# The 16 by 16 substitution of a chunked RWKV-7 kernel, on GpSimd instead of VectorE

## The chip, the cores and the metric

The kernel runs on one core of a Trainium2 chip. The metric is the device time of one execution in microseconds (us), the median over several runs. A core has five engines that run side by side, each taking its own instructions in order: TensorE (PE in the profile; PEld is its loading of weights), VectorE (DVE), ScalarE (ACT), GpSimd (POOL) and SyncE (SP), which here only issues DMAs. The order within each engine's queue is settled when the program is built; between engines semaphores keep the data right.

## The reference

One layer of a hybrid diffusion backbone over 256 latent and 256 context tokens of width 2048, all in float32. A modulated RMS norm is followed by one input projection, whose columns go to an RWKV-7 branch that runs over the tokens in both directions, to a latent attention branch, and to gates. Both branches are projected back, merged by sigmoid gates, projected once more and added to the input. The change lies in the RWKV-7 branch, which per head and direction runs this recurrence over tokens:

```
def rwkv7_step(S, xs):
    r, w, k, v, kk, akk = xs
    sa = einsum("dbhij,dbhj->dbhi", S, -kk)
    S = S * w[..., None, :] + sa[..., :, None] * akk[..., None, :] + v[..., :, None] * k[..., None, :]
    return S, einsum("dbhij,dbhj->dbhi", S, r)
```

There are 16 heads of 64 channels. The recurrence starts at zero, runs through the context, and then from the state reached through the latent tokens.

## The kernel before, in words

The input projections are matrix products in float32 split into a high and a low part (three products for one): ScalarE casts the high part `wh` of a loaded weight tile `w`, VectorE subtracts to get `wl`, and the products go to PSUM as `acc`. The weights come in 512 KB loads on SP's queue into three buffers, and the split halves into three buffers each (`weights`, lines 210 to 219).

The recurrence is done in chunks of 64 tokens. Within a chunk it needs the inverse of a triangular 64 by 64 matrix for each head and direction. The heads go in eight pairs, and each pair in two halves, first the 256 context tokens and then the 256 latent ones, so there are 16 halves. One half has eight chunks counting both directions, two heads, and four diagonal blocks of 16 by 16 in each matrix: 64 blocks. Four generators work on the halves:

- `front(h)` (lines 646 to 813) prepares decays and keys and the triangular products `AQ`, mostly on VectorE and ScalarE (tiles `En`, `Ep`, `th`, `km`, `BK`, `QR` or `Qbd`).
- `diagonal(h, AQ, WT)` (lines 815 to 852) inverts the diagonal blocks. Eight DMAs bring the blocks of `AQ` to DRAM (`dl`, line 821), another brings them back as `ln` with one block to a partition: 64 partitions of 256 elements. Two copies put them into the first half of the tile `wt`, called `X`, those of the backward direction transposed. Then come 14 steps, each with one multiplication into `pr` and one addition into `X`, on 64 partitions and k times (15 - k) elements (14 to 56), and a memset writes the unit diagonal. ScalarE writes the transposed blocks into the other half of `wt` (line 839). One DMA takes both to DRAM (`dw`, line 842), and eight bring them to their places in `WT` (line 848). There is one buffer for `wt`, and `pr` uses the buffer of `ln`.
- `back(h)` (lines 858 to 977) forms the whole inverse from the diagonal blocks with four rounds of products in PSUM tile `lv`, the first two of which read `WT`, and then goes through the chunks with small products (`chp`) and copies (`xs`, `UV`, `Mn`) on ScalarE and VectorE.
- `final(p, Y)` normalizes the result.

In between, a background of input projections (`bg_k`, `bg_r`, `bg_z`, `merge_gate_g` and others) fills TensorE. The order in which all this is written into the program comes from `drive` (lines 505 to 538), a planner with a clock: `Elementwise` objects (lines 110 to 123) stand for VectorE (`V`) and ScalarE (`S`); a call advances the engine's time by elements per partition/rate plus a fixed part (line 121) and sets when a chain's next step may be placed. `diagonal` also gives fixed waits for its DMAs (`LT`, line 60), and `back(h)` is not begun before `diagonal(h)` is through. The instructions of the substitution are written under `tc.high_priority(HS)`, by which the tile framework puts them ahead of others in their engine's queue as soon as they can run.

After the RWKV-7 stage come latent attention, the branch projections and the output projection; they do not use the substitution.

Of the kernel before, what the change touches and what calls it, by code (L numbers as in the profile page):

```python
# [13 lines left out]
ALU = mybir.AluOpType  # L14
# [112 lines left out]
def hybrid_block(  # L127
# [20 lines left out]
    nc = tc.nc  # L148
    clock = Clock()
    V, S = Elementwise(nc.vector, clock, 960, 0.066), Elementwise(nc.scalar, clock, 1200, 0.08)  # L150
    E = Tensor(nc.tensor, clock)
    PSUM = bass.MemoryType.PSUM

# [10 lines left out]
    def con(name):  # L164
        o, w = CO[name]
        return cc[:, o:o + w]
# [54 lines left out]
    def mm3(ps, ah, al, bh, bl, start, stop):  # L221

        E.matmul(ps, lhsT=ah, rhs=bh, start=start, stop=False)
        E.matmul(ps, lhsT=ah, rhs=bl, start=False, stop=False)
        E.matmul(ps, lhsT=al, rhs=bh, start=False, stop=stop)

# [16 lines left out]
    with tc.tile_pool(name="p1", bufs=2) as p1:  # L243
# [20 lines left out]
        def mod_a(k):  # L264

            pm = pp.tile([P, 512], F32, name="pm", tag="ch")
            for r, wm in enumerate(load_mod(k)):
                for g in range(4):
                    E.matmul(pm[32 * g:32 * g + 32, 0:256], lhsT=ssil[:, 4 * r + g], rhs=wm[:, g],
                             start=r == 0, stop=r == 3, tile_position=(0, 32 * g))  # L270
# [4 lines left out]
        def mod_b(k):  # L275

            pm, part = parts.pop(k)
            for i in range(2):
                E.transpose(pm[:, 256 + 128 * i:384 + 128 * i], part[:, 128 * i:128 * i + 128], ident)
            mod = p1.tile([P, 4], F32, name="mod", tag="mod", bufs=4)  # L280
# [10 lines left out]
        for k in range(KT):  # L291
# [3 lines left out]
            else:  # L295
                V.tensor_tensor(sq, xT[:, k], xT[:, k], ALU.mult)
            g = k % 4
            E.matmul(pst[32 * g:32 * g + 32], lhsT=con("ones")[:, 0:32], rhs=sq, start=k < 4, stop=k >= KT - 4,
                     tile_position=(0, 32 * g))
# [205 lines left out]
    def drive(chains, *queues, dens=0.0, lf=1.0, lat=0.0):  # L505

        clock.t = clock.ready = V.t = S.t = 0.0
        chains = [[g, 0.0, None] for g in chains]  # L510
        while chains or any(queues):
            for q in queues:
                if q and not any(c[0] is q[0] for c in chains):
                    chains.append([q[0], clock.t, None])
            for c in chains:
                if c[2] is not None and c[2]():
                    c[2] = None
                    c[1] = max(c[1], clock.t)
                if c[2] is None and clock.t >= c[1] and (clock.density(WIN) >= dens or not (main or extra)):
                    clock.ready = clock.t  # L520
                    r = next(c[0], "end")
                    if r == "end":
                        chains.remove(c)
                        for q in queues:
                            if q and c[0] is q[0]:
                                q.pop(0)
                    else:
                        c[1] = clock.t + lf * (clock.ready - clock.t) + lat
                        if callable(r):
                            c[2] = r  # L530
                        else:
                            c[1] += r or 0.0
                    break
            else:
                t = clock.ready = clock.t
                next(bg, None)
                if clock.t == t:
                    clock.t += 0.2
# [11 lines left out]
    with tc.tile_pool(name="rw", bufs=1) as rw:  # L550
# [95 lines left out]
        def front(h):  # L646
# [104 lines left out]
            else:  # L751
                for d in range(2):
# [6 lines left out]
                    yield  # L759

            lanes.append(diagonal(h, AQ, WT))


# [51 lines left out]
        def diagonal(h, AQ, WT):  # L815

            dl = dram.tile([8, 8, 16, 16], F32, name="dl", tag="dl")
            for g in range(2):
                for b in range(4):
                    r0 = 64 * g + 16 * b  # L820
                    nc.sync.dma_start(dl[:, 4 * g + b].rearrange("u r c -> r u c"), AQ[r0:r0 + 16, g, :, 16 * b:16 * b + 16])
            yield LT[0]
            ln = rw.tile([64, 16, 16], F32, name="ln", tag="ln")
            nc.sync.dma_start(ln.rearrange("p r c -> p (r c)"), dl.rearrange("u h r c -> (u h) (r c)"))
            yield LT[1]
            with tc.high_priority(HS):
                wt = rw.tile([64, 2, 16, 16], F32, name="wt")
                X = wt[:, 0]
                V.tensor_copy(X[0:32], ln[0:32])
                V.tensor_copy(X[32:64], ln[32:64].rearrange("p r c -> p c r"))  # L830
                pr = rw.tile([64, 16, 16], F32, name="pr", tag="ln")
                for k in range(14, 0, -1):

                    m = 15 - k
                    V.tensor_tensor(pr[:, 0:k, 0:m], X[:, 0:k, k:k + 1].to_broadcast([64, k, m]),
                                    X[:, k, k + 1:16].unsqueeze(1).to_broadcast([64, k, m]), ALU.mult)
                    V.tensor_tensor(X[:, 0:k, k + 1:16], X[:, 0:k, k + 1:16], pr[:, 0:k, 0:m], ALU.add)
                V.memset(X.rearrange("p r c -> p (r c)")[:, 0:256:17], 1.0)
                S.copy(wt[:, 1], X.rearrange("p r c -> p c r"))
            dw = dram.tile([2, 8, 8, 16, 16], F32, name="dw", tag="dw")  # L840
            yield LT[2]
            nc.sync.dma_start(dw.rearrange("w u h r c -> (u h) w (r c)"), wt.rearrange("p w r c -> p w (r c)"))
            yield LT[3]
            WTu = WT.rearrange("p w u t -> p (w u) t")
            for g in range(2):
                for b in range(4):
                    r0 = 64 * g + 16 * b
                    nc.sync.dma_start(WTu[r0:r0 + 16, :, 16 * b:16 * b + 16],
                                      dw[:, :, 4 * g + b].rearrange("w u r c -> r (w u) c"))
            yield LT[4]  # L850
            nonlocal inverted
            inverted += 1
# [205 lines left out]
        def back_chain():  # L1058
            nonlocal backs
            for h in range(2 * NPAIR):  # L1060
                yield (lambda: fronts > h and inverted > h)
                yield from back(h)
                backs += 1

        drive([back_chain(), front_chain()], finals, lanes, dens=DENS, lf=LF, lat=LATX)
        while ("q", 3) not in done:
            next(bg)
# [447 lines left out]
```

## Time and profile before

| What | Value |
|---|---|
| Median of 3 runs | 1336.67 us (1335.77 to 1337.12) |
| The profiled execution, its own time | 1337.52 us |
| Its span in the profile | 1335.6 us |
| ScalarE busy | 618.8 us, 46% |
| GpSimd busy | 3.3 us, 9 instructions |
| Mean granted TensorE clock | 0.981 |
| First and last substitution instruction | 172.4 us and 904.0 us |

The page of a profile gives the busy time of each engine in one execution, a timeline in 40 slices, the chain of work that ended last, and the costliest groups of instructions: line, engine, operation, out<-in by the names of the tiles, shapes, count, busy time, mean duration in ns, idle time of the engine just before them and what ended it. Most rows have L122 or L103, since all vector, scalar and matrix operations are issued through helpers there; so tiles tell them apart. Further views give the busy time in chosen windows, who waited for whom, the instructions of one tile, and the instructions in order of time. Matmuls are pipelined and their ends are modelled.

### The profile page before, as it was taken

The numbers are of one execution on the slowest core, as the hardware profiler recorded it, in microseconds if no ns is written. First come the engines' busy times: TensorE is split into PE (matmuls) and PEld (weight loads), VectorE is DVE, ScalarE is ACT, GpSimd is POOL, SyncE is SP. The second block draws the span as 40 slices with busy tenths as digits, with TensorE's granted clock in tenths as the row PEclk, the third lists the DMA queues.
The fourth block names the chain that finished last, engine by engine and source line by source line (L and its number), as shares of the span: only waits on it lengthen the run. The fifth ranks groups of instructions, "written<-read, shape, count | busy, mean of one in ns | idle before, by whom it ended". The sixth has DMA issues, their size and how long they took to land.

```text
span 1335.6 us, 29638 instructions
## 1 busy us (share of the span) xinstructions
PE 1273.5 (95%) x11484; PEld 1057.0 (79%) x11484; DVE 958.0 (72%) x2704; ACT 618.8 (46%) x1370; POOL 3.3 (0%) x9
## 2 busy tenths in 40 slices
PE   5999989999999998999999999999989999799998
PEld 2667877788787787788787777788878888799887
DVE  4445878878777868677876887776548877677655
ACT  3445544444443544344444444544436665444443
POOL 0000000000000000000000000000000000000000
PEclk9999999999999999999999999999979999899999
DMA  9995554354352454254254232353344332577685
GB/s 380 417 418 206 181 164 130 89 171 142 78 173 64 123 163 127 56 166 132 57 110 125 72 99 80 93 151 100 107 150 123 103 103 95 189 227 234 188 270 174
DMA packets 127740, 208.12 MB, mean 156 GB/s; under 512 B 63600, under 2 KB 80752, under 8 KB 127088
## 3 DMA queue, kind: packets, MB, share of 16 engines
q1 hardware_dynamic: 127600, 206.23, 49.0%
q8 instruction: 90, 1.47, 0.5%
q14 instruction: 50, 0.41, 0.1%
HBM read 193.33 MB, written 12.85 MB: 154 GB/s over the span
## 4 chain that ended last, share of the span: by engine, by line
PE 79%; DVE 11%; DMA 6%; issue 2%; ACT 2%; SPq 0%; DVEq 0%; ACTq 0%
PE acc L103 33%; PE chp L103 17%; PE lv L103 10%; PE wk L103 6%; PE a L103 5%; PE ch L103 3%; DMA w<-in_w_proj 3%; DVE wl L122 3%; PE wk L107 2%; PE pm L103 2%; DMA wm<-in_w_mod_ss 2%; DVE BK L122 1%; ACT wh L122 1%; DVE wt L122 1%; DMA xT<-in_xcT 1%
## 5 line engine op out<-in xcount | busy, mean ns | idle before, releaser
L122 ACT CAST wh<-w 128x512 fp32r<-128x512 f32 (+1 forms) x484 | 289.1, 607 | 336.3 <-PE acc L103 182.5
L122 DVE TENSOR_TENSOR wl<-w,wh 128x512 fp32r<-128x512 f32 (+1 forms) x480 | 319.7, 674 | 134.1 <-ACT wh L122 123.8
L103 PE MATMUL acc<-hmh,wh 128*128 128x256 f32 (+1 forms) x1200 | 390.6, 325 | 0.0
L103 PE MATMUL acc<-hml,wh 128*128 128x256 f32 (+2 forms) x1200 | 370.3, 309 | 0.8 <-issue 0.8
L103 PE MATMUL acc<-hmh,wl 128*128 128x256 f32 (+1 forms) x1184 | 364.6, 308 | 0.6 <-DVE wl L122 0.5
L103 PEld LDWEIGHTS acc<-hmh,wh 128*128 128x128 f32 x1200 | 228.0, 190 | 28.7 <-issue 6.8
L103 PEld LDWEIGHTS acc<-hmh,wl 128*128 128x128 f32 x1184 | 225.3, 190 | 14.9 <-DVE wl L122 1.1
L103 PEld LDWEIGHTS acc<-hml,wh 128*128 128x128 f32 (+1 forms) x1200 | 228.0, 190 | 11.0 <-issue 0.8
L122 DVE TENSOR_TENSOR pr<-wt 64x14 f32<-64x14 f32 (+6 forms) x224 | 42.5, 190 | 4.7
L122 DVE TENSOR_TENSOR wt<-wt,pr 64x14 f32<-64x14 f32 (+6 forms) x224 | 42.3, 189 | 4.3
L122 ACT COPY UV<-Mn 64x128 f32<-64x128 f32 x112 | 33.1, 295 | 22.1 <-DVE Mn L122 18.4
L103 PE MATMUL chp<-ob0h,wh 128*128 128x256 f32 x128 | 37.4, 293 | 5.7 <-ACT ob0h L122 5.7
L103 PEld LDWEIGHTS chp<-UV,AQ 128*64 128x64 f32 (+1 forms) x512 | 24.5, 138 | 21.3 <-ACT UV L122 10.9
L103 PE MATMUL a<-hmh,wh 128*128 128x512 f32 x96 | 40.7, 424 | 0.0
L122 ACT COPY UV<-chp 64x128 f32<-64x128 f32 x64 | 16.5, 257 | 50.8 <-PE chp L103 50.6
L103 PE MATMUL chp<-UV,AQ 128*64 128x64 f32 (+1 forms) x512 | 35.9, 238 | 4.2 <-ACT UV L122 4.1
L103 PE MATMUL a<-hmh,wl 128*128 128x512 f32 x96 | 38.1, 397 | 0.4 <-DVE wl L122 0.4
L103 PE MATMUL a<-hml,wh 128*128 128x512 f32 x96 | 37.9, 395 | 0.0
L103 PE MATMUL chp<-ob0l,wh 128*128 128x256 f32 x128 | 37.4, 292 | 0.0
L122 DVE SCALAR_TENSOR_TENSOR Mn<-chp,rho,Mr 128x64 f32<-128x64 f32 x96 | 24.1, 278 | 18.2 <-PE chp L103 17.7
L103 PE MATMUL chp<-ob0h,wl 128*128 128x256 f32 x128 | 37.1, 290 | 0.0
L103 PE MATMUL chp<-ob1h,wh 128*128 128x256 f32 x128 | 36.5, 285 | 0.0
(324 smaller groups left out, 2388.1 us busy)
## 6 DMA issues: line engine op xcount, KB each, us to landing
w<-in_w_proj SPq DMA_DIRECT2D x148, 512.0 KB, 3.8
wm<-in_w_mod_ss SPq DMA_DIRECT2D x64, 512.0 KB, 9.4
w<-in_w_mod_g SPq DMA_DIRECT2D x32, 512.0 KB, 3.6
w<-in_w_br SPq DMA_DIRECT2D x32, 512.0 KB, 3.6
w<-in_w_out SPq DMA_DIRECT2D x32, 512.0 KB, 3.7
w<-in_w_first SPq DMA_DIRECT2D x16, 384.0 KB, 8.5
xT<-in_xcT SPq DMA_DIRECT2D x4, 1024.0 KB, 8.6
thd<-th SPq DMA_DIRECT2D x32, 128.0 KB, 1.8
```

Source lines behind the costliest of these rows:

```text
L103: return self.engine.matmul(out, lhsT=lhsT, rhs=rhs, **kw)
L107: return self.engine.transpose(*a)
L122: return fn(out, *a, **kw)
```

## The change

The planner gets a third `Elementwise` object, `G`, for GpSimd, with VectorE's rate and fixed part. The two copies, the 28 multiplications and additions and the memset of each substitution are issued through it. ScalarE's transposing copy, the DMAs, the tiles and their buffers, the priority and the fixed waits stay.

```
+    G = Elementwise(nc.gpsimd, clock, 960, 0.066)
...
-        clock.t = clock.ready = V.t = S.t = 0.0
+        clock.t = clock.ready = V.t = S.t = G.t = 0.0
...
-                V.tensor_copy(X[0:32], ln[0:32])
-                V.tensor_copy(X[32:64], ln[32:64].rearrange("p r c -> p c r"))
+                G.tensor_copy(X[0:32], ln[0:32])
+                G.tensor_copy(X[32:64], ln[32:64].rearrange("p r c -> p c r"))
                 pr = rw.tile([64, 16, 16], F32, name="pr", tag="ln")
                 for k in range(14, 0, -1):
                     m = 15 - k
-                    V.tensor_tensor(pr[:, 0:k, 0:m], X[:, 0:k, k:k + 1].to_broadcast([64, k, m]),
+                    G.tensor_tensor(pr[:, 0:k, 0:m], X[:, 0:k, k:k + 1].to_broadcast([64, k, m]),
                                     X[:, k, k + 1:16].unsqueeze(1).to_broadcast([64, k, m]), ALU.mult)
-                    V.tensor_tensor(X[:, 0:k, k + 1:16], X[:, 0:k, k + 1:16], pr[:, 0:k, 0:m], ALU.add)
-                V.memset(X.rearrange("p r c -> p (r c)")[:, 0:256:17], 1.0)
+                    G.tensor_tensor(X[:, 0:k, k + 1:16], X[:, 0:k, k + 1:16], pr[:, 0:k, 0:m], ALU.add)
+                G.memset(X.rearrange("p r c -> p (r c)")[:, 0:256:17], 1.0)
                 S.copy(wt[:, 1], X.rearrange("p r c -> p c r"))
```

## The prediction

> **What bounds the kernel now.** I began with the page: the span, busy time by engine, then the costliest groups.
>
> ```profile
> span 1335.6 us, 29638 instructions
> ...
> PE 1273.5 (95%) x11484; PEld 1057.0 (79%) x11484; DVE 958.0 (72%) x2704; ACT 618.8 (46%) x1370; POOL 3.3 (0%) x9
> ...
> L122 DVE TENSOR_TENSOR pr<-wt 64x14 f32<-64x14 f32 (+6 forms) x224 | 42.5, 190 | 4.7
> L122 DVE TENSOR_TENSOR wt<-wt,pr 64x14 f32<-64x14 f32 (+6 forms) x224 | 42.3, 189 | 4.3
> ```
>
> TensorE bounds the kernel, and GpSimd does nothing after its first memsets. The work that moves is 448 small VectorE instructions of 0.19 us. Taking it off an engine that is 72% busy gains only what TensorE now waits for because of it. So the next view was busy time by window: all of the stage from the first substitution to the last, and then the sixteen stretches in which a substitution runs, one per half (a half is one pair of heads with the context or the latent tokens).
>
> ```profile
> 172.40:904.00 731.60, 704.50 (x7293) 576.38 (x7293) 567.87 (x1742) 326.45 (x782) 0.00 (x0) 0.98 0.41 116
> ```
>
> ```profile
> 172.40:190.30 17.90, 13.79 (x119) 12.07 (x119) 15.80 (x61) 6.29 (x13) 0.00 (x0) 0.90 0.58 170
> ...
> 250.50:264.80 14.30, 14.08 (x135) 10.82 (x132) 13.27 (x47) 8.43 (x21) 0.00 (x0) 1.00 0.25 76
> ...
> 343.20:354.80 11.60, 11.26 (x161) 8.78 (x161) 10.45 (x43) 4.67 (x11) 0.00 (x0) 1.00 0.16 48
> ...
> 483.90:496.50 12.60, 12.60 (x129) 11.47 (x129) 10.89 (x44) 4.99 (x11) 0.00 (x0) 1.00 0.67 206
> ...
> 691.00:706.70 15.70, 11.94 (x109) 10.63 (x108) 9.65 (x41) 4.49 (x11) 0.00 (x0) 0.92 0.53 109
> 757.60:768.00 10.40, 10.40 (x136) 8.09 (x134) 9.51 (x40) 4.72 (x10) 0.00 (x0) 1.00 0.09 35
> ...
> sum 222.70, PE 212.43 PEld 177.25 DVE 196.70 ACT 99.67 POOL 0.00; mean PE 13.28 PEld 11.08 DVE 12.29 ACT 6.23 POOL 0.00
> ```
>
> After each window's length come the busy times of PE, PEld, DVE, ACT and POOL. VectorE is 196.70/222.70 = 88% busy in these stretches and (567.87 - 196.70)/(731.60 - 222.70) = 73% outside them, so it is crowded where the substitution runs. TensorE is idle 222.70 - 212.43 = 10.3 us in all sixteen: 4.1 in the first, 3.8 in the one from 691, where VectorE itself is idle 6 us and so isn't the cause, and 2.4 in the other fourteen. A substitution takes 222.70/16 = 13.9 us on average, though its own instructions are much shorter: it is interleaved with other VectorE work.
>
> **What it removes.** The tile that the substitution works on shows all its instructions:
>
> ```profile
> L122 DVE COPY wt<-ln x32: 271/324/381, 172.4 to 890.6; 32x256 f32<-32x256 f32 x32
> L122 DVE MEMSET wt<- x16: 72/72/72, 174.3 to 892.5; 64x16 f32 x16
> ```
>
> Per half VectorE loses 28 x 0.19 + 2 x 0.324 + 0.072 = 6.0 us, 97 us over 16 halves. What TensorE gets of that I take from the first stretch, where one wait makes up the whole loss.
>
> ```profile
> 181.91 0.70 PE L103 MATMUL wk<-QR,BK 64*128 64x128 f32 x4 [4.11 <-DVE pr L122]
> ```
>
> ```profile
> 181.09 0.67 DVE L122 TENSOR_TENSOR QR<-cr,Ep 128x512 f32<-128x512 f32 x1
> ```
>
> ```profile
> 172.40:181.09 8.69, 2.43 (x13) 0.00 (x0) 1.00 0.60 182
> ```
>
> The matmul needs the QR tile, whose last part VectorE starts at 181.09. Up to there the instructions that read or write the substitution's tile took 2.43 us of VectorE (this window counts them alone). With them gone QR is ready 2.4 us earlier, and the wait falls from 4.1 to 1.7. The next thing late there is the rest of VectorE's own queue. I take the same share, 2.43/4.11 = 0.59, of the 2.4 us idle in the fourteen other stretches: 1.4. The 3.8 of the stretch from 691 stay. Gain: 2.4 + 1.4 = 3.8 us, bounded above by 10.3 (all the idle time) and below by zero if nothing else happens.
>
> **What it adds.** GpSimd runs 31 instructions per half, most of which wait for the one before. No operation with an input runs on GpSimd in this trace; its memsets are the nearest rows.
>
> ```profile
> L554 POOL MEMSET WT<- 128x1024 f32 x2 | 1.8, 954 | 127.0 <-PE a L103 127.0
> ...
> L562 POOL MEMSET restart<- 128x260 f32 x1 | 0.3, 313 | 0.0
> L563 POOL MEMSET restart<- 128x4 f32 x1 | 0.1, 104 | 0.1
> ```
>
> A memset of 16 elements would take 0.104 + 12 x (0.313 - 0.104)/256 = 0.114 us here, against 0.072 on VectorE. Lower bound: 28 x 0.114 + 2 x 0.313 + 0.114 = 3.9 us for the substitution. Estimate: VectorE's two-input instruction takes 0.190/0.072 = 2.6 times its memset, so on GpSimd 0.30 us. For the handing over between dependent instructions I read VectorE where nothing stands between two of them:
>
> ```profile
> 694.05 0.20 DVE L122 TENSOR_TENSOR wt<-wt,pr 64x44 f32<-64x44 f32 x1
> 694.28 0.20 DVE L122 TENSOR_TENSOR pr<-wt 64x50 f32<-64x50 f32 x1
> ```
>
> 0.23 from start to start for 0.20 of work, so 0.03 more, 0.33 per instruction. Two copies at 0.45 (between the 0.31 of a memset of that size and twice it): 28 x 0.33 + 0.9 + 0.1 = 10.2 us. Upper bound: each instruction also waits out one whole instruction of VectorE, the commonest being the split of weights:
>
> ```profile
> L122 DVE TENSOR_TENSOR wl<-w,wh 128x512 fp32r<-128x512 f32 (+1 forms) x480 | 319.7, 674 | 134.1 <-ACT wh L122 123.8
> ```
>
> 28 x (0.33 + 0.674) + 1 = 29 us. I take 10 to 16 us, near the estimate, the top being it with a 0.3 chance of meeting such an instruction (28 x 0.3 x 0.674 = 5.7; 0.3 is its share of VectorE's work, 319.7/958.0, at 88% busy). That is about the 13.9 us of today. [...]
>
> **Who waits for its end.** The order is: ScalarE's transposing copy, the DMA to dw, eight DMAs to WT, then TensorE's level products lv<-WT,AQ.
>
> ```profile
> 193.56 3.76 SPq L848 DMA_DIRECT2D WT<-dw  x8
> ```
>
> ```profile
> 198.06 0.32 PE L103 MATMUL lv<-WT,AQ 64*64 64x64 f32 x2
> ```
>
> ```profile
> 269.81 3.77 SPq L848 DMA_DIRECT2D WT<-dw  x8
> ```
>
> ```profile
> 279.56 0.56 PE L103 MATMUL lv<-WT,AQ 64*64 64x64 f32 x10
> ```
>
> ```profile
> 567.93 3.77 SPq L848 DMA_DIRECT2D WT<-dw  x8
> ```
>
> ```profile
> 602.46 0.74 PE L103 MATMUL lv<-WT,AQ 64*64 64x64 f32 x18
> ```
>
> ```profile
> DMA to landing us min/median/max: 1.9/2.2/5.1
> ```
>
> In the half of the last pair of rows, a typical one, the blocks have landed at about 567.93 + 3.77 + 2.2 = 573.9 and are used at 602.46: 28.6 us to spare, which hide even the upper bound. The third half has 279.56 - (269.81 + 3.77 + 2.2) = 3.8 us to spare on a substitution of 14.3. In the first 193.56 + 3.76 + 2.2 = 199.5 lies behind the first use at 198.1, so I count none to spare there, on 17.9. So a chain of up to 17.9 us costs nothing there. At 29 us the first would be 11.1 late and the third 29 - 14.3 - 3.8 = 10.9, some 22 us together.
>
> Two engines that do other work also stand in line. ScalarE takes its instructions in order, and its copy (line 839) waits for the substitution's end with weight casts, copies of UV and the exponentials behind it. SP's queue holds the DMA to dw, with weight loads behind it. Where the copy stands was settled when the program was built. This is what such waits cost today:
>
> ```profile
> 354.88 0.64 ACT L122 COPY wt<-wt 64x256 f32<-64x256 f32 x1 [3.69 <-DVE wt L122]
> ```
>
> ```profile
> 496.52 0.63 ACT L122 COPY wt<-wt 64x256 f32<-64x256 f32 x1 [2.77 <-DVE wt L122]
> ```
>
> ```profile
> SPq L842 <- ACT wh L122: 13.1, 1, 13.1
> ```
>
> ScalarE held for 3.69 and 2.77 us, and TensorE lost 0.34 and 0.00 us in those stretches; SP was held up to 13.1 us (in the stretch from 757.6) and TensorE lost nothing. So some 3.7 us of ScalarE's waiting are covered by three buffers of split weights. Without the cover a wait costs TensorE its own length.
>
> The kernel's own planner (lines 505 to 538) no longer counts the substitution to VectorE: 28 x 0.066 + 1120/960 and 0.75 for the copies and the memset, 3.8 us per half by its formula in line 121. It will place some later steps earlier, which shifts the order on TensorE by a little either way. I price that at zero, within 2 us either way (half of one half's 3.8). GpSimd's own queue has nothing behind the substitution, and the buffer that ln and pr share comes free long before the next half's load, halves being some (757.60 - 172.40)/12 = 49 us apart.
>
> Sum against the profiled execution's 1337.52 us (span 1335.6 and 1.92 around it): 1337.52 - 3.8 = 1333.7. The runs' median, 1336.67, lies 0.85 lower, so the forecast is 1332.9. A difference under 0.2%, 2.7 us, can hardly be told from none here.
>
> **Rival one: VectorE gets nothing back.** GpSimd and VectorE may hold each other up, so that 6 us less of work is paid for by as much waiting. For it: 28 reading instructions per half beside an engine that is 88% busy; if each held a VectorE instruction for 6.0/28 = 0.21 us, less than the 0.30 that I give one of them, nothing is left. Against it: not each meets one, and VectorE also reads PSUM and writes with one input. Time: 1336.7. [...] It is also the case in which the change doesn't do what it says.
>
> **Rival two: slower, ScalarE's queue held.** If the substitution on GpSimd ends X us after the place that the copy was given in ScalarE's order, everything behind the copy waits, in each of 16 halves, and TensorE loses about X - 3.7 per half. It decides from X = 3.7. With X = 5.7, the meetings with VectorE that the order can't foresee, that is 16 x 2.0 = 32 us less the 3.8 gained: 1336.7 + 28 = 1365. For it: GpSimd's two-input time stands in no row, VectorE's crowding adds to it, and all sixteen halves repeat it. Against it: on VectorE the substitution is drawn out by the work between its steps and by VectorE's own waits, which a separate engine doesn't have, so its end may also come early.
>
> **How the numbers follow.** The gain as worked out: 0.42. Nothing to be seen, by rival one or the planner's shift: 0.20. Rival two, with the first and third halves' lateness in it: 0.38. The likeliest case alone reaches from 1326 (10.3 less) to 1334. The range of all three is 1326 to 1366: it leaves out 0.04 below, where more than the idle time would have to go, and 0.16 above, X of 6 us and more.
>
> **What would show it.** Right: no substitution on DVE, POOL busy 150 to 260 us in 448 two-input instructions; chains of 10 to 16 us; the wait of wk<-QR,BK near 182 down to 1 or 2 us; VectorE under 75% busy in the same stretches; ScalarE's copy waiting under 4 us for POOL. Wrong: two-input instructions of over 0.5 us on POOL; wl<-w,wh longer than 0.674 (rival one); ScalarE's copy waiting 6 us and more for POOL, with TensorE idle right behind it (rival two); level products waiting for WT in the first halves.

## The result and the profile after

The changed kernel takes 1401.19 us (median of 4 runs, 1399.39 to 1403.34) against 1336.89 (4 runs) for the kernel before: a ratio of 1.0474, 95% interval 1.0448 to 1.0499. It is slower by 64 us, where 1332.9 was forecast, and also beyond the 1365 of rival two.

From the page of the kernel after, the span, the busy time by engine and the rows of the moved work (count, then busy time and mean ns of one, then the engine's idle time just before):

```profile
span 1398.7 us, 29644 instructions
...
PE 1302.0 (93%) x11484; PEld 1081.7 (77%) x11484; DVE 887.7 (63%) x2208; ACT 616.8 (44%) x1370; POOL 157.2 (11%) x505
...
L122 DVE TENSOR_TENSOR wl<-w,wh 128x512 fp32r<-128x512 f32 (+1 forms) x480 | 322.3, 680 | 216.7 <-ACT wh L122 209.4
...
L122 POOL TENSOR_TENSOR pr<-wt 64x14 f32<-64x14 f32 (+6 forms) x224 | 68.0, 304 | 17.6
L122 POOL TENSOR_TENSOR wt<-wt,pr 64x14 f32<-64x14 f32 (+6 forms) x224 | 66.7, 298 | 16.6
L122 ACT COPY wt<-wt 64x256 f32<-64x256 f32 x16 | 9.9, 622 | 91.8 <-POOL wt L122 91.8
```

The work moved as meant: VectorE falls from 958.0 to 887.7 us, and GpSimd's instructions take 0.30 us. The span grew by 63.1 us, and the two PE entries split it. TensorE is busy 28.5 us more with the same 11,484 matmuls, and idle 1398.7 - 1302.0 = 96.7 us instead of 62.1, which is 34.6 more.

The last row names the new wait. The waits of ScalarE on the substitution, first of the kernel before, then after (total, times, longest):

```profile
ACT wt L122 <- DVE wt L122: 14.7, 10, 3.7
```

```profile
ACT wt L122 <- POOL wt L122: 91.8, 16, 7.5
```

All sixteen copies now wait, 91.8/16 = 5.7 us each. That isn't because the substitution became longer. Busy times of each engine from its first instruction to the start of ScalarE's copy, as sums over the 16 halves, before and then after:

```profile
sum 224.60, PE 214.33 PEld 178.97 DVE 197.23 ACT 101.34 POOL 0.00; mean PE 13.40 PEld 11.19 DVE 12.33 ACT 6.33 POOL 0.00
```

```profile
sum 189.30, PE 163.78 PEld 136.14 DVE 81.29 ACT 50.38 POOL 153.62; mean PE 10.24 PEld 8.51 DVE 5.08 ACT 3.15 POOL 9.60
```

The stretch shrank from 224.60/16 = 14.0 us to 11.8. But ScalarE has only 3.15 us of work in it, where it had 6.33: the copy stands further forward in ScalarE's order, and what used to run ahead of it is now behind it. In the sixth half of the kernel before, the copies UV and AQ ran first, and the copy of wt hardly waited:

```profile
395.53 0.36 ACT L122 COPY UV<-wk 64x256 f32<-64x256 f32 x1 [0.42 <-PE wk L107]
...
396.88 0.62 ACT L122 COPY AQ<-Qbd 64x512 f32<-64x512 f32 x1
...
399.75 0.63 ACT L122 COPY wt<-wt 64x256 f32<-64x256 f32 x1 [0.58 <-DVE wt L122]
```

How this reaches TensorE can be read in the same half of after, where the copy of wt comes ahead of UV (start, duration, engine, operation; in brackets the idle time before it and what ended it):

```profile
411.57 0.27 ACT L122 COPY Y<-chp 128x128 f32<-128x128 f32 x1 [0.65 <-PE chp L103]
...
418.24 0.62 ACT L122 COPY wt<-wt 64x256 f32<-64x256 f32 x1 [6.40 <-POOL wt L122]
418.88 0.36 ACT L122 COPY UV<-wk 64x256 f32<-64x256 f32 x1
419.28 0.43 DVE L122 COPY UV<-wk 64x256 f32<-64x256 f32 x1 [6.98 <-ACT UV L122]
419.74 0.69 DVE L122 TENSOR_TENSOR Z<-lv,cc 128x512 f32<-128x512 f32 x1
...
420.49 1.97 PE L103 MATMUL lv<-WT,Z 64*64 64x64 f32 x32 [5.82 <-DVE Z L122]
```

ScalarE stands for 6.40 us before the copy. UV is next in its queue, then AQ. VectorE's next instruction waits for that copy of UV and stands for 6.98. The Z behind it in VectorE's queue, which had nothing to do with the substitution, is what TensorE's next product needs, and TensorE stands for 5.82. From 414.67, where TensorE's last product ends, to 418.24 GpSimd is the only one of the five engines at work. So TensorE's waits between 165 and 965 us changed in kind, first before, then after:

```profile
PE wk L103 <- DVE QR L122: 5.5, 6, 1.8
PE wk L103 <- DVE BK L122: 5.1, 1, 5.1
PE chp L103 <- ACT UV L122: 4.9, 5, 2.9
PE wk L103 <- DVE pr L122: 4.1, 1, 4.1
```

```profile
PE lv L103 <- DVE Z L122: 21.2, 4, 7.0
PE chp L103 <- ACT UV L122: 14.4, 6, 6.2
PE chp L103 <- DVE UV L122: 10.6, 4, 5.0
PE wk L107 <- ACT BKT L122: 5.2, 1, 5.2
...
PE lv L103 <- DMA WT<-dw: 1.7, 1, 1.7
PE acc L103 <- DVE wl L122: 1.5, 4, 0.7
```

The big waits are for small tiles of the recurrence. For split weights (acc<-wl) TensorE waits 1.5 us in all.

The other part of the loss is the clock. Windows of after (length; busy us of PE, PEld, DVE, ACT, POOL; the granted clock follows POOL's count): a stretch that begins where one stall of 5.19 us ends, then two stretches each from the start of ScalarE's hold to 4 us past its copy, and the sum over the sixteen:

```profile
319.00:323.60 4.60, 4.60 (x45) 3.93 (x45) 1.70 (x4) 1.03 (x3) 0.00 (x0) 0.50 0.57 149
```

```profile
411.84:422.86 11.02, 5.20 (x81) 4.65 (x80) 3.44 (x7) 2.87 (x7) 5.01 (x18) 0.83 0.07 15
...
470.47:482.47 12.00, 10.77 (x139) 8.96 (x139) 4.92 (x9) 4.25 (x9) 5.70 (x22) 1.00 0.33 93
...
sum 165.74, PE 109.40 PEld 88.89 DVE 59.83 ACT 49.88 POOL 71.72; mean PE 6.84 PEld 5.56 DVE 3.74 ACT 3.12 POOL 4.48
```

Behind that stall TensorE is busy all the time at a granted clock of 0.50; the stretches of 0.50 in this trace last 3.41 us or a multiple of it. Each stretch of reduced clock times the part of the clock withheld makes, over the execution, 25.6 us before and 52.9 after: 27.3 more, about the 28.5 us by which TensorE's busy time grew. That the two are the same time is inferred from their sizes. In this trace each of TensorE's thirteen stalls of 2.27 us or more behind its first product has a stretch of 0.50 that begins within it or at most 0.48 us behind its end; these thirteen make 46.1 of the 52.9 us. In the hold stretches TensorE is idle 165.74 - 109.40 = 56.3 us. It isn't even: the hold before 477.85 lasted 7.4 us and cost 1.23, the one before 418.24 lasted 6.4 and cost 5.82. In the stretch of the first the granted clock was 1.00, in that of the second 0.83.

SP is held too: its waits before the DMA to dw add up to 66.3 us in the kernel before and to 140.0 after. Which of the two queues costs the time is a question for the experiments.

### The profile page after: what moved, and what is told of

It reads as the page before. It is cut to its first block, busy times and chain, and to the rows that moved or that the text cites. A ratio compares the mean times of both kernels' runs of the same rounds, so it can differ in the third digit from the quotient of the medians.

```text
span 1398.7 us, 29644 instructions
## 1 busy us (share of the span) xinstructions
PE 1302.0 (93%) x11484; PEld 1081.7 (77%) x11484; DVE 887.7 (63%) x2208; ACT 616.8 (44%) x1370; POOL 157.2 (11%) x505
## 4 chain that ended last, share of the span: by engine, by line
PE 66%; POOL 11%; DVE 7%; DMA 7%; issue 4%; ACT 3%; SPq 2%; POOLq 0%; DVEq 0%; ACTq 0%
PE acc L103 25%; PE chp L103 14%; PE lv L103 9%; POOL wt L122 6%; PE wk L103 6%; PE a L103 5%; POOL pr L122 5%; DMA ln<-dl 3%; PE ch L103 3%; DVE wl L122 2%; PE pm L103 2%; PE wk L107 2%; ACT wh L122 1%; SPq L822 1%; DMA w<-in_w_proj 1%
## 5 line engine op out<-in xcount | busy, mean ns | idle before, releaser
L103 PE MATMUL acc<-hmh,wh 128*128 128x256 f32 (+1 forms) x1200 | 397.9, 332 | 2.0 <-ACT wh L122 1.2
L122 POOL COPY wt<-ln 32x256 f32<-32x256 f32 x32 | 18.2, 569 | 631.9 <-DMA ln<-dl 583.2
L122 POOL TENSOR_TENSOR pr<-wt 64x14 f32<-64x14 f32 (+6 forms) x224 | 68.0, 304 | 17.6
L122 POOL TENSOR_TENSOR wt<-wt,pr 64x14 f32<-64x14 f32 (+6 forms) x224 | 66.7, 298 | 16.6
L122 ACT COPY wt<-wt 64x256 f32<-64x256 f32 x16 | 9.9, 622 | 91.8 <-POOL wt L122 91.8
L103 PEld LDWEIGHTS chp<-UV,BKT 128*64 128x64 f32 x448 | 22.3, 140 | 32.6 <-DVE UV L122 12.1
L103 PE MATMUL chp<-UV,BKT 128*64 128x64 f32 x448 | 33.2, 241 | 13.7 <-DVE UV L122 10.2
L122 ACT COPY UV<-chp 64x128 f32<-64x128 f32 x64 | 16.5, 257 | 62.5 <-PE chp L103 62.1
L122 DVE COPY xs<-chp 128x128 f32<-128x128 f32 x64 | 18.5, 290 | 38.6 <-PE chp L103 38.3
L103 PE MATMUL lv<-WT,Z 64*64 64x64 f32 x512 | 22.5, 250 | 21.2 <-DVE Z L122 21.2
L103 PEld LDWEIGHTS lv<-WT,Z 64*64 64x64 f32 x512 | 20.0, 161 | 25.2 <-DVE Z L122 22.4
```

What stands on the lines that cost most here:

```text
L103: return self.engine.matmul(out, lhsT=lhsT, rhs=rhs, **kw)
L122: return fn(out, *a, **kw)
```

## The experiments

The theory: the time is set by which in-order queues the chain holds, ScalarE's first and SP's behind it, and not by how long GpSimd takes or how much it holds VectorE up. The rivals: that GpSimd and VectorE hold each other up ('ports' in the expectations); the planner's shifted order; the lateness of WT. Each ratio is to the kernel before on the same chip, with its 95% interval. Two accounts of the planner occur: the old one, in which the substitution is booked on VectorE's object (and the copy on ScalarE's) wherever it runs, and the new one with the separate object `G`.

**The copy on another engine.** The copy, alone, goes to GpSimd, where nothing stands behind it.

```
-                S.copy(wt[:, 1], X.rearrange("p r c -> p c r"))
+                G.tensor_copy(wt[:, 1], X.rearrange("p r c -> p c r"))
```

> The kernel after, with the transposing copy of wt moved from ScalarE to GpSimd too, so that no engine with other work waits for the substitution's end. Theory (ScalarE's queue is held for 5.7 us in each half, and TensorE stalls and drops its clock behind it): ScalarE waits for no wt, TensorE's idle time between 165 and 965 us falls from 70 to under 30 us, granted clock back to 0.98, time 1328 to 1342 us. Rival 'planner' (VectorE no longer counted, another order on TensorE): still 1385 us or more. Rival 'ports' (VectorE and GpSimd hold each other up): still 1385 us or more.

Measured: 1341.88 us, 1.0057 (1.0022 to 1.0092). Moving one instruction per half takes away 4.17 of the 4.74%, some 56 of the 64 us, with the substitution still on GpSimd. TensorE's idle time between 165 and 965 us fell from 69.8 to 35.4 us, where under 30 was expected. (The planner now books the copy on `G` too; a run further down leaves it on ScalarE and comes out the same.) The same line with `V.tensor_copy` moves the wait to VectorE's queue:

> The kernel after, with the transposing copy on VectorE instead of ScalarE. Theory (any queue with other work that is held costs as much): VectorE is held for some 5 us per half with the splits of weights behind it, time 1370 to 1420 us. Rival 'it is ScalarE's own work, its UV copies and casts, that matters': below 1355 us. Rivals 'planner' and 'ports': about 1400 us too, so this run does not tell those apart from the theory.

Measured: 1402.3 us, 1.0500 (1.0470 to 1.0530), and VectorE now waits for the substitution:

```profile
DVE wt L122 <- POOL wt L122: 90.9, 16, 7.8
```

As much waiting, as much time: it matters that an engine with other work stands, not whether that is ScalarE or VectorE.

**The copy later in ScalarE's queue.** First the copy is written 9 us of the planner's time later, without the priority:

```
-                S.copy(wt[:, 1], X.rearrange("p r c -> p c r"))
+            yield 9.0
+            S.copy(wt[:, 1], X.rearrange("p r c -> p c r"))
```

> The kernel after, with the transposing copy still on ScalarE, but written 9 us later by the planner's clock and without priority, so that other ScalarE work stands ahead of it. Theory: the place of the copy in ScalarE's order is what costs, so its wait falls from 5.7 us to under 2 us on average and the time to 1332 to 1350 us (the blocks come 5 us later than in the version with the copy on GpSimd). Rivals 'planner' and 'ports': 1385 us or more, since substitution and planner are untouched.

Measured: 1395.7 us, 1.0451 (1.0430 to 1.0471), and ScalarE's wait stayed (102.7 us in 16). The edit was a miss: the place in the queue wasn't moved by where the instruction is written. It was then tied behind the ScalarE instruction that the planner had issued last:

```
+            yield 9.0
+            last = getattr(S.last, "ins", S.last)
+            with tc.issue_after(last):
```

> The kernel after, with the transposing copy still on ScalarE, but queued by an ordering edge behind the last ScalarE instruction that is written by then, 9 us later by the planner's clock. Theory (the place of the copy in ScalarE's order costs): ScalarE's wait for wt falls from 92 us in all to under 30 us, and the time to 1332 to 1352 us. Rival 'GpSimd beside VectorE costs, and the copy on GpSimd only happened to help': the wait falls, but the time stays over 1380 us.

Measured: 1342.19 us, 1.0052 (1.0037 to 1.0067), inside the range, with ScalarE's wait halved, where under 30 us was expected:

```profile
ACT wt L122 <- POOL wt L122: 46.5, 11, 7.2
```

The copy stays on ScalarE and nine tenths of the loss are gone. What cost the time was its place in the order. Half of the waiting is still there and only a tenth of the loss, so the sum of ScalarE's waits does not give the price.

**The planner's account.** The substitution stays on VectorE, and only the account changes:

```
-    G = Elementwise(nc.gpsimd, clock, 960, 0.066)
+    G = Elementwise(nc.vector, clock, 960, 0.066)
```

> The kernel before as to engines (the substitution on VectorE), with the planner's accounts of the kernel after (the substitution is not counted to VectorE). Theory: the order matters little, 1331 to 1343 us. Rival 'planner': 1360 us or more, most of the 64 us that were lost.

Measured: 1324.80 us, 0.9918 (0.9898 to 0.9937). Little change was expected; the shift of the order alone gains 11 us. Then the change under the old account (a small class `Counted` issues on GpSimd and books on VectorE's object):

```
-    G = Elementwise(nc.gpsimd, clock, 960, 0.066)
+    G = Counted(nc.gpsimd, V)
```

> The kernel after (substitution on GpSimd, copy on ScalarE), with the planner's accounts of the kernel before: the substitution is counted to VectorE as if it ran there. Theory (ScalarE is held whatever the plan): 1385 to 1420 us, with over 70 us of ScalarE waiting for wt. Rival 'the new plan and the wait only together': under 1370 us.

Measured: 1404.01 us, 1.0522 (1.0489 to 1.0556). The loss doesn't come from the account; ScalarE waits 95.2 us in 16 here too. With the copy on GpSimd as well, under the old account:

```
+    G, GC = Counted(nc.gpsimd, V), Counted(nc.gpsimd, S)
...
+                GC.tensor_copy(wt[:, 1], X.rearrange("p r c -> p c r"))
```

> Substitution and transposing copy on GpSimd, planned as in the kernel before (substitution counted to VectorE, copy to ScalarE). Theory (no engine with other work waits, only the engines differ from the kernel before): 1328 to 1345 us. If the 17 us by which the copy on GpSimd is behind the kernel with the new plan and the substitution on VectorE come from GpSimd beside VectorE (the ports): 1345 to 1360 us.

Measured: 1368.02 us, 1.0247 (1.0230 to 1.0264), above both of the expected ranges. And with the new account, the substitution on VectorE and the copy on GpSimd:

> Substitution on VectorE, planner's accounts as in the kernel after, and only the transposing copy on GpSimd. Theory: ScalarE's remaining wait of 9 us for wt goes, TensorE's stalls hardly change against the kernel with the new plan alone (1325 us): 1318 to 1328 us. If GpSimd reading beside VectorE costs much even for one instruction per half: over 1330 us.

Measured: 1324.16 us, 0.9915 (0.9900 to 0.9929), the same as with the copy on ScalarE. So under the old account 32 us were still lost with the copy away from ScalarE.

**The second queue.** In that kernel (the 1368.0 us one) SP waits for the substitution at the DMA to dw. Its wait, and then one stretch of its timeline (SPq rows are DMA issues):

```profile
SPq L859 <- POOL wt L138: 153.1, 16, 19.2
```

```profile
682.61 0.62 SPq L859 DMA_DIRECT2D dw<-wt  x1
685.62 3.74 SPq L865 DMA_DIRECT2D WT<-dw  x8
689.46 6.19 SPq L230 DMA_DIRECT2D w<-in_w_proj  x4
693.35 1.14 ACT L122 CAST wh<-w 128x512 fp32r<-128x512 f32 x2 [8.07 <-DMA w<-in_w_proj]
694.00 1.29 DVE L122 TENSOR_TENSOR wl<-w,wh 128x512 fp32r<-128x512 f32 x2 [7.50 <-ACT wh L122]
...
696.41 0.69 PE L103 MATMUL chp<-UV,BKT 128*64 128x64 f32 x8 [7.98 <-DVE UV L122]
```

The weight load is issued only behind dw and WT, at 689.46; ScalarE stands 8.07 us for it, VectorE 7.50 for ScalarE, TensorE 7.98 for a UV behind that. To test it, the chain's DMAs go to GpSimd's own queue, under the new account and then under the old:

```
-            nc.sync.dma_start(dw.rearrange("w u h r c -> (u h) w (r c)"), wt.rearrange("p w r c -> p w (r c)"))
+            nc.gpsimd.dma_start(dw.rearrange("w u h r c -> (u h) w (r c)"), wt.rearrange("p w r c -> p w (r c)"))
...
-                    nc.sync.dma_start(WTu[r0:r0 + 16, :, 16 * b:16 * b + 16],
+                    nc.gpsimd.dma_start(WTu[r0:r0 + 16, :, 16 * b:16 * b + 16],
```

> Substitution and transposing copy on GpSimd as in the run with the copy there (1342 us, SP held 150 us for dw), and the DMA to dw and the eight to WT issued from GpSimd's queue instead of SP's. Theory, extended (SP's queue, with weight loads behind the DMA to dw, is the second one that is held): SP waits for no wt any more, and the time falls to 1318 to 1332 us, unless GpSimd needs so long to issue nine DMAs per half that WT comes late (then level products wait for WT and the time stays at 1340 us or more). Rival 'ports' (the remaining loss is GpSimd beside VectorE): 1338 to 1345 us with no waits for WT.

> The substitution and the transposing copy on GpSimd with the old planner's account (the kernel that took 1368.0), and now also the DMA to dw and the eight to WT issued on GpSimd's own queue, so that nothing of this chain stands in ScalarE's or SP's order any more. If SP's held queue is what costs 32 us in that kernel over the old one, this one comes back to 1335 to 1350, with the waits of wh for w and of wl for wh near 690 gone and TensorE idle under 35 us between 165 and 965 us. [...] The issues on GpSimd may themselves make WT late in the first and third half, by up to 15 us together, and that is inside the first range.

Measured: 1328.67 us, 0.9945 (0.9922 to 0.9968), under the new account, and 1322.75 us, 0.9916 (0.9883 to 0.9949), under the old. The second is 44 us less, by the ratios, than with the DMAs on SP, and 12 below the lowest time expected of it: taking the chain's DMAs out of SP's queue is worth all of the 32 us, and more. The wait and the nine issues left SP together, so what each was worth isn't separated. The price on GpSimd's queue shows in the kernel with the new account, in its page and in TensorE's waits:

```profile
L849 POOL DMA_DIRECT2D WT<-dw x128 | 71.5, 566 | 47.8 <-DMA dw<-wt 10.9
```

```profile
PE lv L103 <- DMA WT<-dw: 16.4, 2, 10.7
```

An issue there takes 0.57 us, and the first and the third half, which had the least to spare, wait 5.7 and 10.7 us for WT. Two tries to hold back only the DMA to dw in SP's order, by the same sort of edge that had worked for the copy (`DQ` is SP's queue, its last DMA kept in mind), told little:

```
+            yield 9.0
+            with tc.issue_after(getattr(DQ.last, "ins", DQ.last)):
```

> Substitution and transposing copy on GpSimd, planner's accounts of the kernel after; the DMA to dw stays on SP, but 9 us later by the planner's clock and behind the last SP instruction written by then. Theory, extended: SP's wait for GpSimd falls from 150 us to under 40 us and the time to 1316 to 1332 us. Rival 'ports': 1338 to 1345 us.

> Substitution and copy on GpSimd, planner's accounts of the kernel before (1368 us, SP held 153 us), with the DMA to dw 9 us later by the planner's clock and behind the last SP instruction written by then. Theory, extended: most of the 32 us between that run and the kernel before go, 1330 to 1346 us. Rival 'ports': 1360 us or more.

Measured: 1368.21 us, 1.0251 (1.0232 to 1.0271), new account, and 1370.82, 1.0277 (1.0260 to 1.0293), old account. SP's wait at dw fell only to 125.7 and 142.5 us, where under 40 us was expected of the first, so the edge didn't do what it was for. Why the first became 26 us slower by it stays open.

**Rival 'ports'.** To the kernel with the copy on GpSimd (1341.88), GpSimd repeats the 28 instructions on a scratch tile, after the result is ready:

```
+                w2 = rw.tile([64, 128], F32, name="w2")
+                for k in range(14, 0, -1):
+                    ...
+                    nc.gpsimd.tensor_tensor(y, X[:, 0:k, k:k + 1].to_broadcast([64, k, m]),
+                                            X[:, k, k + 1:16].unsqueeze(1).to_broadcast([64, k, m]), ALU.mult)
+                    nc.gpsimd.tensor_tensor(y, X[:, 0:k, k + 1:16], y, ALU.add)
```

> The run with substitution and copy on GpSimd (1342 us), and behind them in each half the 28 two-input instructions once more, on a scratch tile that nobody reads: GpSimd's load beside VectorE is doubled, no wait is added. Theory (the ports cost little, since GpSimd pays for most collisions): 1338 to 1350 us. Rival 'ports': the 5 to 30 us that GpSimd beside VectorE costs come once more, 1350 to 1375 us.

Measured: 1344.62 us, 1.0070 (1.0039 to 1.0101), which can't be told from 1.0057; VectorE's busy time rose from 890.6 to 897.3 us. By the two intervals, doubling the GpSimd work beside VectorE costs at most some 8 us; that the two engines hold each other up is not where 64 us went.

**What VectorE's relief is worth.** The best version so far differs from the kernel before in three moves. Two controls take them apart: the kernel before with nothing changed but the queue of the nine DMAs, and the 1322.75 us version with the substitution alone back on VectorE:

```
-    G, GC = Counted(nc.gpsimd, V), Counted(nc.gpsimd, S)
+    G, GC = Counted(nc.vector, V), Counted(nc.gpsimd, S)
```

> The kernel before, with nothing changed but the queue of the DMA to dw and the eight to WT, GpSimd's instead of SP's; substitution on VectorE, copy on ScalarE. If the 11.5 us by which the version with everything on GpSimd beats the old kernel come from VectorE's 97 us of relief, this one stays at the old time, 1331 to 1340. If they come from taking the chain's DMAs out of SP's order (SP is held at dw for 66 us in the old kernel), this one is as fast as that version, 1320 to 1327, and the relief of VectorE is worth nothing.

> The version with everything on GpSimd under the old planner's account (1322.75 us), with the substitution alone put back on VectorE; copy and DMAs stay on GpSimd. It differs from that version in the 31 instructions per half only. If the relief of VectorE is what gains, this one is slower than it by 4 to 12 us, 1327 to 1335, with the wait of wk for QR near 182 back at about 4 us. If freeing ScalarE and SP from the chain is what gains, it is within 3 us of 1322.75.

Measured: 1335.43 us, 1.0001 (0.9986 to 1.0017), and 1342.00, 1.0042 (1.0027 to 1.0058). The DMAs' queue alone gains nothing on balance; it also made TensorE wait 5.3 us for WT in the first half, which the kernel before doesn't do. The last run is slower than the 1327 to 1335 expected of it: between it and the 1322.75 us version, which differ in the 31 instructions alone, lie 1.0042 - 0.9916 = 1.26%, 17 us. Against the kernel before, the whole move gains 0.84%, 11 us. In the first stretch the wait that the prediction began with shows it, with the substitution on VectorE and then on GpSimd:

```profile
182.27 1.23 PE L103 MATMUL wk<-QR,BK 64*128 64x128 f32 x8 [4.11 <-DVE pr L138]
```

```profile
179.19 0.68 PE L103 MATMUL wk<-QR,BK 64*128 64x128 f32 x6 [0.94 <-DVE QR L122]
```

And the page of the 1322.75 us version:

```profile
span 1320.8 us, 29706 instructions
...
PE 1271.8 (96%) x11484; PEld 1054.3 (80%) x11484; DVE 887.8 (67%) x2208; ACT 611.3 (46%) x1354; POOL 263.4 (20%) x665
```

TensorE is idle 1320.8 - 1271.8 = 49.0 us, 13.1 less than in the kernel before.

**A mixed version.** New account; in the first three halves, which wait for WT, substitution and copy run on VectorE with their DMAs on SP, from the fourth on all of it is GpSimd's:

```
+            G.engine = nc.vector if h < 3 else nc.gpsimd
+            dma = nc.sync if h < 3 else nc.gpsimd
```

> The planner's account as changed; in the first three halves, where the level products wait for WT, the substitution and the copy run on VectorE and their DMAs stay on SP's queue; from the fourth half on substitution, copy and DMAs are GpSimd's. If the time is set by which in-order queues the chain holds and by the first and third halves' lack of slack, this is faster than both kernels, 1312 to 1326, with no TensorE wait for WT. If taking the work off VectorE is worth nothing in itself, it comes to the 1324 to 1325 of the kernels with the substitution on VectorE and this account. Above 1328.7 (everything on GpSimd in all halves) the account of the first and third halves is wrong.

Measured: 1321.37 us, 0.9891 (0.9851 to 0.9931), with no wait of TensorE for WT. It beats both kernels and can't be told from the 1322.75 us version. Nor can it be told from the kernel before with only the account changed (0.9918), so under the new account a gain from VectorE's relief isn't shown, and the gain of the account and that of the relief don't add up.

## Why the prediction was wrong, point by point

**GpSimd's own times: right.** Forecast 0.30 us per two-input instruction and chains of 10 to 16 us; measured 0.304 and 0.298 us, and 10.7 to 16.0 us, mean 11.8. That 0.30 was met is partly luck: it was meant for an instruction alone, which took 0.255 us, and the rest of the mean is meetings with VectorE. **WT's slack: right.** TensorE waited for WT once, 1.7 us. **Rival one, that VectorE gets nothing back: not borne out.** Its wl<-w,wh went from 0.674 to 0.680 us only, its busy time fell by 70.3 us, and the doubled GpSimd work cost at most some 8 us.

**The step that failed** is "So some 3.7 us of ScalarE's waiting are covered by three buffers of split weights", and with it that rival two was not taken as the likeliest. It had X = 5.7 as an example, and X was 5.7 in the mean, which is luck: the example came from meetings with VectorE that lengthen the chain, the 5.7 measured from the copy's earlier place. Of the 91.8 us that ScalarE waited, a cover of 3.7 in each half would have left some 33 to TensorE; in the hold stretches it stood idle for 56.3. Two things in the step didn't hold:

- The cover was read off two waits that seemed to cost nothing, and put down to the weight buffers. Those cover the projections' products, and they did: 1.5 us of waits for wl. TensorE's order also holds the recurrence's small products, whose Z, UV and BKT have nothing in reserve. They pass through ScalarE, or through VectorE behind an instruction that needs ScalarE. A hold of 6.4 us cost 5.82 in one half, while one of 7.4 cost 1.23 in another, where TensorE had projection products to go on with. No constant cover held.
- The price had no term for the clock. TensorE's idle time over the whole execution grew by 34.6 us, near the 16 x 2.0 = 32 of rival two (the near agreement is partly luck: 56.3 lie in the hold stretches, and less idle time elsewhere offsets some). The 28.5 us of slower matmuls behind the stalls are the missing term: 1336.7 + 34.6 + 28.5 = 1399.8.

The stretches in which those two waits were read end at 354.80 and 496.50, where the two copies begin, so what stood behind the copies was not in them. Behind the first TensorE lost nothing up to 359. Behind the second it stood for a UV, in the kernel before already:

```profile
498.40 0.33 PE L103 MATMUL chp<-AR,UV 128*64 128x64 f32 x2 [0.52 <-ACT UV L122]
```

**"Its end may also come early"** was given against rival two. It did: the stretch is 2.2 us shorter. The copy waits all the same, since its place was set anew when the program was built, with 3.2 us less of ScalarE's work ahead of it. Why the builder places it there, whether it takes GpSimd for faster than it is, isn't shown by a trace; that the place decides is shown by the copy tied further back.

**SP's hold, by which "TensorE lost nothing"**, was judged in the same way, by the loads that stood behind it then. In the changed kernel SP stood 140.0 us at dw, but little of the 64 us is its: with the copy moved SP stood 150.2 us, and 0.57% was left. With the copy out of the way, having the chain's DMAs on SP cost 15 us under the new account (1.0057 to 0.9945) and 44 under the old (1.0247 to 0.9916). Why the same hold (150.2 and 153.1 us in all) costs so much less under one account stays open, beyond that other loads stand behind it.

**The planner's shift, "zero, within 2 us either way"**: 11 us faster by itself with the substitution on VectorE, 25 us with substitution and copy on GpSimd (1.0247 against 1.0057), and nothing with the DMAs there too (0.9945 against 0.9916, intervals that overlap). Its direction can't be read off the time that it stops counting.

**The gain, 3.8 us, at most 10.3**: under the old account, with no queue held, the relief is worth up to 17 us, beside a control that is itself 0.4% slower than the kernel before for a reason that stays open. The wait of 4.11 near 182 fell by 3.4 instead of 2.4 in the changed kernel already, whose timeline has:

```profile
180.51 0.68 PE L103 MATMUL wk<-QR,BK 64*128 64x128 f32 x6 [0.76 <-DVE QR L122]
```

The bound counted TensorE's idle time in the sixteen stretches alone; work put off there is late in the stretches between, and the clock counts there too: between the two versions that differ in the substitution alone, TensorE's idle time fell by 12.3 us and its busy time by 8.2, at a granted clock of 0.981 with the substitution on VectorE and 0.987 on GpSimd. Not all of that is relief: 2.7 of the 12.3 are TensorE's wait for WT (5.8 us with the substitution on VectorE, 3.1 on GpSimd).

## What to carry to other kernels

When a chain moves to another engine, follow its end to every in-order queue that takes it up, here a copy on ScalarE and a DMA on SP, and move those steps along with it or tie them behind the queue's other work; half a move cost nearly 5% where the whole one, under the same old account, gained 0.8%. Price a hold by what stands behind it in the held queue and by the products of TensorE's order that have no reserve, never by the waits that cost nothing in the old order, and add to TensorE's idle time the slower matmuls behind the longer stalls, here 28.5 us on 34.6. Where a planner's accounts change along with the engine, give the account a run of its own: here it was worth 11 us by itself.

## What the hardware showed that was not expected

GpSimd and VectorE do hold each other up, but GpSimd mostly pays. From the timeline of after, GpSimd's instructions and VectorE's beside them:

```profile
260.21 0.25 POOL L122 TENSOR_TENSOR pr<-wt 64x44 f32<-64x44 f32 x1
...
260.46 0.69 DVE L122 TENSOR_TENSOR wl<-w,wh 128x512 fp32r<-128x512 f32 x1 [0.62 <-ACT wh L122]
260.54 0.75 POOL L122 TENSOR_TENSOR wt<-wt,pr 64x44 f32<-64x44 f32 x1
...
261.36 0.29 POOL L122 TENSOR_TENSOR pr<-wt 64x50 f32<-64x50 f32 x1
...
261.44 0.69 DVE L122 TENSOR_TENSOR W<-WT,lv 128x512 f32<-128x512 f32 x1 [0.29 <-PE lv L103]
```

Beside wl<-w,wh, with both inputs in SBUF, an addition takes 0.75 us instead of the 0.27 that one of its shape takes alone; beside W<-WT,lv, which reads lv from PSUM, a multiplication takes 0.29 instead of 0.28. Of all 448, about 82 overlap a VectorE instruction with two SBUF inputs and take 0.49 us in the mean; about 101 run beside other VectorE work and take 0.27, the rest 0.255. In the other direction, about 45 of the 128x512 wl<-w,wh overlap GpSimd's work and take 0.74 us, the others 0.689: some 2.3 us in all, against 19 on GpSimd. Some 82 meetings that cost 0.23 us each, over 16 halves, lengthened a chain by about 1.2 us, which is less than the copy's 5.7 us wait.

A DMA issue on GpSimd's queue took 0.57 us of that engine, and the length of a stall wasn't its full price: after the one of 5.19 us that ended at 318.93 the granted clock stayed at 0.50 for 4.6 us more, though TensorE had work.
